# A hand-written instruction order at the two token-by-token passages of a two-layer encoder trunk

## The chip, the core and the metric

The kernel runs on one core of one Trainium2 chip. The metric is the device time of one execution, in microseconds (us). The profile is that of one execution, with the start and duration of every instruction on each engine: TensorE (PE, with its weight loads apart as PEld), VectorE (DVE), ScalarE (ACT), GpSimd (POOL) and SyncE (SP, which here only issues transfers).

## The reference

x is 256 tokens of 2048 float32 numbers. Two layers follow one another; cut to what matters here:

```python
for l in range(DEPTH):                      # 2 layers
    h = rms_norm(x, pre_mix_norm[l])
    m = hybrid_mixer(h, ...)                # h @ w_in, two kinds of attention, mix @ w_o
    x = x + rms_norm(m, post_mix_norm[l])
    h = rms_norm(x, pre_ffn_norm[l])
    f = (silu(h @ w_gate[l]) * (h @ w_up[l])) @ w_down[l]
    x = x + rms_norm(f, post_ffn_norm[l])
```

`rms_norm(m, post)` needs the sum of squares over all 2048 columns of a token before any column of it can be added to x, and the next projection needs x transposed (features on partitions). So at "output projection to gate and up" and at "down projection to the next layer's input projection" everything that follows waits for the last column of a token. The two passages occur three times: the first in both layers, the second once, between them.

## The kernel before

**Numbers.** Every float32 matrix product is made of three matmuls. Each operand is split in two: `hi`, its rounding to the matmul's format, made by ACT, and `lo`, what is left (operand minus `hi`), made by DVE. The product is hi times hi, hi times lo, and lo times hi.

**Weights.** All weights are one stream of 128x1024 pieces in the order of use (`weight_order`). `fetch(upto)` issues their transfers on SP's queue into four `raw` buffers; `feed(upto)` makes each piece's `hi` (ACT, L307) and `lo` (DVE, L317), with six buffers of each. A `hi` can be made when its raw piece has landed and PE has finished with an older piece's buffer; a raw buffer is free when its `lo` is made. In the gate and up columns after the first, some `lo` are made by POOL (`helped`, L310). Some products use a seven-product scheme for a 2x2 block (`seven_products`, L1084 to L1086, with sums of weights `T` and `G` made at L279 to L291); in the passages only plain products occur.

**Tokens.** The 256 tokens are two blocks of 128 (t = 0 and 1). The 2048 output columns of a projection are four columns c of 512. The last two columns (2 and 3) are accumulated last, and their last pairs of rows are done token block by token block: first both columns of block 0, then both of block 1, so that block 0 can be normed while PE works on block 1.

**At a passage**, for each block: an accumulator is added to a shared part (`evac_sum`, L589; in the output projection block 1's shared part was added before), ACT squares it and sums (L586, L591), DVE multiplies it by the norm's gain (L587, L592), `rescale` turns the four sums into 1/rms (ACT's Ln and Exp at L602 and L603, a Newton step in two DVE instructions, L476 and L477), and DVE adds the scaled columns to x (L627). `transposed` then turns four 128x128 parts of x on PE into one bank (L485), ACT rounds them with the next norm's gain (L488, tiles xF or xI) and DVE makes their `lo` (L493). `inv_rms` squares the new x (ACT, L512) for the next norm; the result is applied behind the next projection. The next projection's first column (gate and up: `eight`, L1250; input projection: `eight_in`, L1084 to L1086 through `product`) starts with two pairs of rows of block 0, then the same of block 1, then both blocks together. Its banks are those of the accumulators.

**Order.** A planner puts each engine's instructions in order at build time by its own estimate of when they are ready; `tc.high_priority` moves instructions forward, `tc.manual_schedule(engines=...)` keeps the written order on the named engines, `tc.issue_after(ins)` queues an instruction behind another one, and `behind()` uses that for a given number of following `lo` (the list `held`). Engines work their queue in order. Before, the output projection's passage is in written order on ACT and DVE up to block 1's last column, which is left to the planner with high priority (L1184 to L1202). The down passage (L1398 to L1420) is left to the planner, with high priority for the evacuations and rescales.

Of the kernel before, what the change touches and what calls it, by code (L numbers as in the profile page):

```python
# [17 lines left out]
P = 128  # L18
D = 2048
S = 256  # L20
L = 2
# [146 lines left out]
def kernel(  # L168
# [128 lines left out]
    def feed(upto):  # L297
        fetch(upto)
        while fed[0] < min(upto, len(stream)):
# [7 lines left out]
            nc.scalar.activation(hi, raw, AF.Copy)  # L307
# [13 lines left out]

    rests = []
    held = [None, 0]
    follows, newest_rest = {}, {}
# [154 lines left out]

    def transposed(t, g0, tiles, cols=range(4)):  # L480
        for cg in cols:
            pb = acc_bank(f"xT_ps{t}_{cg}")
            for j in range(4):
                k = cg * 4 + j
                nc.tensor.transpose(pb[:, j * P : (j + 1) * P], x_part(t, k * P, P), ident)  # L485
            for j in range(4):
                k = cg * 4 + j
                rounded = nc.scalar.activation(  # L488
                    tiles[k][:, 0, t * P : (t + 1) * P], pb[:, j * P : (j + 1) * P], AF.Copy, scale=gains[:, g0 + k : g0 + k + 1]
                )  # L490
            for j in range(4):
                k = cg * 4 + j
                rest = nc.vector.scalar_tensor_tensor(  # L493
                    out=tiles[k][:, 1, t * P : (t + 1) * P],
                    in0=pb[:, j * P : (j + 1) * P],
                    scalar=gains[:, g0 + k : g0 + k + 1],
                    in1=tiles[k][:, 0, t * P : (t + 1) * P].bitcast(F32),
                    op0=ALU.mult,
                    op1=ALU.subtract,
                )  # L500
        return rounded, rest
# [4 lines left out]
    def inv_rms(t, pool, nm, parts=None):  # L506
        ss = small.tile([P, 1], F32, tag="ssx", name=f"ssx_{nm}_{t}")
        part = small.tile([P, 4], F32, tag="ssp", name=f"ssp_{nm}_{t}")
        for h in range(4):
            if parts is None:  # L510
                junk = pool.tile([P, CW], F32, tag="t2", name=f"junk_{nm}_{t}_{h}")
                nc.scalar.activation(junk, x_part(t, h * CW, CW), AF.Square, accum_out=part[:, h : h + 1])  # L512
            else:
                nc.scalar.activation(parts[h], parts[h], AF.Square, accum_out=part[:, h : h + 1])
# [66 lines left out]

    def evac_sum(pool, acc, mg, ssm, gpost, c, t, nm, summed=False):
        m = mg[t, c // 2][:, c % 2, :]
        if summed:
            junk = pool.tile([P, CW], F32, tag="t2", name=f"jm_{nm}_{t}_{c}")
            nc.scalar.activation(junk, acc, AF.Square, accum_out=ssm[t][:, c : c + 1])  # L586
            nc.vector.tensor_tensor(out=m, in0=acc, in1=gpost[:, c * CW : (c + 1) * CW], op=ALU.mult)  # L587
            return
        nc.vector.tensor_tensor(out=m, in0=acc, in1=m, op=shared_sign(t, c % 2))  # L589
        junk = pool.tile([P, CW], F32, tag="t2", name=f"jm_{nm}_{t}_{c}")  # L590
        nc.scalar.activation(junk, m, AF.Square, accum_out=ssm[t][:, c : c + 1])  # L591
        nc.vector.tensor_tensor(out=m, in0=m, in1=gpost[:, c * CW : (c + 1) * CW], op=ALU.mult)  # L592

    def rescale(mg, ssm, t, nm, then=None, newest=None):
        halves = newest is not None
# [5 lines left out]
        nc.vector.tensor_scalar(out=half, in0=three, scalar1=-0.5 / D, scalar2=-0.5 * EPS, op0=ALU.mult, op1=ALU.add)  # L601
        nc.scalar.activation(u, fourth, AF.Ln, scale=1.0 / D, bias=most)  # L602
        nc.scalar.activation(r, u, AF.Exp, scale=-0.5)  # L603
        nc.vector.tensor_scalar(out=ms, in0=fourth, scalar1=-0.5 / D, scalar2=half, op0=ALU.mult, op1=ALU.add)
        newton(r, u, ms)
        if halves:
# [8 lines left out]
        for c in range(4):  # L615
            if halves and c == 0:
                continue
            if halves and c == 3:
# [7 lines left out]
            sl = x_part(t, c * CW, CW)  # L626
            nc.vector.scalar_tensor_tensor(  # L627
                out=sl, in0=mg[t, c // 2][:, c % 2, :], scalar=r, in1=sl, op0=ALU.mult, op1=ALU.add
            )
# [505 lines left out]
    for l in range(L):  # L1135
# [187 lines left out]
        for half in range(2):  # L1323
# [74 lines left out]
            for t in range(NT):  # L1398
# [76 lines left out]
```

## Time and profile before

| | |
|---|---|
| median of 3 runs | 2181.57 us (2181.53 to 2182.7) |
| the profiled execution, whole | 2183.48 us |
| its span in the profile | 2181.7 us |
| granted TensorE clock | 0.999 of full speed |
| PE busy | 2166.0 us (99%), 9944 matmuls |
| PEld busy | 1781.7 us (82%) |
| DVE busy | 1920.7 us (88%), 2657 instructions |
| ACT busy | 1400.4 us (64%), 2089 instructions |
| POOL busy | 260.5 us (12%) |
| DMA | 471.49 MB, mean 216 GB/s |

A row of a timeline gives the start, the duration, the engine, the line of the kernel, the operation, the tiles (output, then inputs), their shapes and the count; in brackets stands how long the engine was idle before it, and what ended that. Matmuls overlap: a row's duration is longer than the distance to the next row. A row of the waits gives who waited for whom, the total, the number of times and the longest, in us.

### The profile page before, as it was taken

To read this page: it belongs to the slowest core of one execution; us is meant where nothing else is said; L and a number is where in the kernel's file an instruction comes from. 1 tells how busy PE (TensorE), PEld (TensorE's weight loads), DVE (VectorE), ACT (ScalarE), POOL (GpSimd) and SP (SyncE) were. 2 spreads that over 40 slices of the span, in tenths; PEclk is the share of its full clock that TensorE was granted. 3 is DMA by queue.
4 is the path that set the end of the run, shared out by engine and by line. 5 is a ranking of instruction groups with operands and counts; after the bars stand their busy time and mean duration, and the time that the engine had idled before them with its cause. 6 is when DMAs were issued, how large, how long until landed. Compare 5 with 4: busy or idle time off the path is not lost.

```text
span 2181.7 us, 28784 instructions
## 1 busy us (share of the span) xinstructions
PE 2166.0 (99%) x9944; PEld 1781.7 (82%) x9944; DVE 1920.7 (88%) x2657; ACT 1400.4 (64%) x2089; POOL 260.5 (12%) x243
## 2 busy tenths in 40 slices
PE   9999999999999999999999999999999999999998
PEld 7888888788888888888878888887888888888886
DVE  7888658899999999999878886589999999999997
ACT  7666665756666656666665666657666666576664
POOL 1100000031222221000010000000212222200000
PEclk9999999999999999999999999999999999999999
DMA  9544555488887767767465555555888877768683
GB/s 323 194 164 174 193 184 176 165 300 234 239 258 229 226 231 233 239 223 258 149 241 174 172 174 188 191 164 191 286 237 241 262 222 227 240 225 244 204 268 100
DMA packets 140851, 471.49 MB, mean 216 GB/s; under 512 B 16016, under 2 KB 17040, under 8 KB 140192
## 3 DMA queue, kind: packets, MB, share of 16 engines
q1 hardware_dynamic: 121952, 436.03, 57.7%
q0 software_dynamic: 18176, 33.07, 9.2%
q8 instruction: 78, 1.28, 0.2%
q14 instruction: 69, 0.57, 0.1%
q10 hardware_dynamic: 576, 0.54, 0.1%
HBM read 461.19 MB, written 8.39 MB: 215 GB/s over the span
## 4 chain that ended last, share of the span: by engine, by line
PE 94%; DVE 3%; ACT 2%; issue 1%; DMA 0%; SPq 0%; DVEq 0%; ACTq 0%
PE c L1250 19%; PE in L1084 7%; PE in L1086 7%; PE in L1085 7%; PE dn L1357 4%; PE dn L1356 4%; PE dn L1359 4%; PE p L1085 3%; PE c L1084 3%; PE p L1084 3%; PE p L1086 3%; PE c L1085 3%; PE c L1086 3%; PE o L569 2%; PE o L571 2%; PE o L570 2%
## 5 line engine op out<-in xcount | busy, mean ns | idle before, releaser
L317 DVE TENSOR_TENSOR lo<-raw,hi 128x1024 fp32r<-128x1024 f32 x468 | 561.9, 1220 | 103.3 <-ACT hi L307 102.3
L307 ACT ACTIVATE hi<-raw 128x1024 fp32r<-128x1024 f32 x490 | 501.5, 1053 | 102.3 <-DMA raw<-in_weights_in_turn_dram 41.8
L1250 PE MATMUL c<-hi,xF 128*128 128x512 f32 x1280 | 345.9, 391 | 1.5 <-DVE xF L493 1.5
L1250 PEld LDWEIGHTS c<-hi,xF 128*128 128x128 f32 x1280 | 238.3, 188 | 50.3 <-DVE xF L493 2.0
L258 POOL DMA_DIRECT2D T<-in_weights_in_turn_dram x126 | 111.2, 883 | 1373.8 <-DMA T<-in_weights_in_turn_dram 716.6
L1250 PE MATMUL c<-lo,xF 128*128 128x512 f32 x640 | 198.2, 390 | 2.5 <-DVE lo L317 2.5
L279 ACT ACTIVATE Th<-G 128x1024 fp32r<-128x1024 f32 x126 | 133.1, 1056 | 79.8 <-DVE G L291 78.6
L281 DVE TENSOR_TENSOR Tl<-G,Th 128x1024 fp32r<-128x1024 f32 x126 | 153.9, 1221 | 10.1 <-ACT Th L279 10.1
L1356 PE MATMUL dn<-hi,jh 128*128 128x512 f32 x416 | 162.0, 389 | 0.0
L1357 PE MATMUL dn<-lo,jh 128*128 128x512 f32 x416 | 161.8, 389 | 0.0
L307 ACT ACTIVATE hi<-G 128x1024 fp32r<-128x1024 f32 x126 | 132.9, 1055 | 44.6 <-DMA G<-in_weights_in_turn_dram 27.8
L281 DVE TENSOR_TENSOR lo<-T,hi 128x1024 fp32r<-128x1024 f32 x126 | 159.6, 1266 | 0.3 <-ACT hi L279 0.2
L279 ACT ACTIVATE Th<-T 128x512 fp32r<-128x512 f32 x126 | 79.7, 633 | 118.6 <-DVE T L290 113.3
L291 DVE TENSOR_TENSOR G<-G,T 128x1024 f32<-128x1024 f32 x126 | 153.5, 1218 | 1.8
L1250 PEld LDWEIGHTS c<-lo,xF 128*128 128x128 f32 x640 | 120.1, 188 | 28.1 <-DVE lo L317 3.0
L317 DVE TENSOR_TENSOR lo<-G,hi 128x1024 fp32r<-128x1024 f32 x108 | 131.6, 1219 | 12.3 <-ACT hi L307 12.2
L279 ACT ACTIVATE hi<-T 128x1024 fp32r<-128x1024 f32 x126 | 132.2, 1049 | 12.1 <-PE c L1086 10.6
L1084 PE MATMUL in<-hi,xT 128*128 128x512 f32 x328 | 131.0, 401 | 0.6 <-DVE xT L862 0.6
L1084 PE MATMUL in<-hi,xI 128*128 128x512 f32 x328 | 131.1, 401 | 0.0
L1085 PE MATMUL in<-lo,xI 128*128 128x512 f32 x328 | 128.0, 390 | 0.3 <-DVE lo L317 0.3
L1085 PE MATMUL in<-lo,xT 128*128 128x512 f32 x328 | 127.8, 391 | 0.4 <-DVE lo L891 0.4
L1359 PE MATMUL dn<-hi,jl 128*128 128x512 f32 x416 | 128.0, 389 | 0.0
(485 smaller groups left out, 4954.2 us busy)
## 6 DMA issues: line engine op xcount, KB each, us to landing
raw<-in_weights_in_turn_dram SPq DMA_DIRECT2D x490, 512.0 KB, 4.6
T<-in_weights_in_turn_dram SPq DMA_DIRECT2D x126, 512.0 KB, 5.3
G<-in_weights_in_turn_dram SPq DMA_DIRECT2D x126, 512.0 KB, 5.4
T<-in_weights_in_turn_dram POOLq DMA_DIRECT2D x126, 256.0 KB, 6.1
GU<-in_weights_in_turn_dram SPq DMA_DIRECT2D x32, 512.0 KB, 6.5
V<-in_weights_in_turn_dram SPq DMA_DIRECT2D x8, 512.0 KB, 3.7
away_ffn<-x SPq DMA_DIRECT2D x8, 512.0 KB, 8.2
xd<-away_ffn SPq DMA_DIRECT2D x8, 512.0 KB, 9.4
```

Source lines behind the costliest of these rows:

```text
L279: nc.scalar.activation(h, w, AF.Copy)
L281: newest_rest[i] = nc.vector.tensor_tensor(out=l, in0=w, in1=h.bitcast(F32), op=ALU.subtract)
L291: nc.vector.tensor_tensor(out=g, in0=g, in1=t2.unsqueeze(1).to_broadcast([P, 2, CW]), op=ALU.add)
L307: nc.scalar.activation(hi, raw, AF.Copy)
L317: rest = nc.vector.tensor_tensor(out=lo, in0=raw, in1=hi.bitcast(F32), op=ALU.subtract)
L1084: nc.tensor.matmul(a, sh, hi, start=first, stop=False, skip_group_check=open_sums[0])
L1085: nc.tensor.matmul(a, sh, lo, start=False, stop=False, skip_group_check=open_sums[0])
L1086: return nc.tensor.matmul(a, sl, hi, start=False, stop=last, skip_group_check=open_sums[0])
L1250: nc.tensor.matmul(a, stat[part], w[j][:, kk, :], start=first and kk + n == 0, stop=last and kk == 1 and n == 2)
L1356: nc.tensor.matmul(accs[c, t], sh, hi[:, kk, :], start=first, stop=False, skip_group_check=open_sums[0])
L1357: nc.tensor.matmul(accs[c, t], sh, lo[:, kk, :], start=False, stop=False, skip_group_check=open_sums[0])
L1359: nc.tensor.matmul(accs[c, t], sl, hi[:, kk, :], start=False, stop=last, skip_group_check=open_sums[0])
```

## The change

Both passages get a written order. In the output projection's passage ACT, DVE and, for the first half, PE follow it; in the down passage of layer 0 ACT and DVE do. The steps that were one function are split (`turned_x`, `rounded_x` and `rest_of_x` out of `transposed`; `squared`, `gained` and `shared_added` out of `evac_sum`; `root_of`, which gives way at two points, and `rescaled` out of `rescale`), so that they can be interleaved one by one. `rounded_next` makes the next weight's `hi` at once and returns a function that makes its `lo` later, on DVE or on a named engine.

In the output projection: the `hi` and `lo` of the sixth weight piece of the passage stand behind the square of block 0's column 2; block 1's matmuls all come before block 0's transposes; one `lo` in each layer is made by POOL, behind the `lo` before it; block 1's gain multiplies stand behind its first two rescales, and read the accumulators until then; the squares of the next norm come behind the rounding of block 1's first columns. In the down passage of layer 0: block 0's norm follows its last column at once, the `hi` and `lo` of the next layer's first four weight pieces stand at chosen places, block 1's first rescale stands ahead of block 0's third and fourth, and the following `lo` are queued behind block 1's rests (`held_next`, two and then four of them) and two `hi` behind block 1's Exp (`rounded_behind`). All steps on the last three row pairs' activations (`prep`) come before the last pairs. The last layer's down passage keeps its order. Cut to its core:

```diff
             hi = wpool.tile([P, 2, CW], F32R, tag="hi", bufs=6, name=f"hi{i}")
-            nc.scalar.activation(hi, raw, AF.Copy)
+            with tc.issue_after(rounded_behind.pop(0).ins) if rounded_behind else nullcontext():
+                nc.scalar.activation(hi, raw, AF.Copy)
...
+    def rounded_next():
+
+        i = fed[0]
+        fetch(i + 1)
+        raw = raws[i]
+        hi = wpool.tile([P, 2, CW], F32R, tag="hi", bufs=6, name=f"hi{i}")
+        nc.scalar.activation(hi, raw, AF.Copy)
+        lo = wpool.tile([P, 2, CW], F32R, tag="lo", bufs=6, name=f"lo{i}")
+        ready[i] = (hi, lo)
+        fed[0] += 1
+
+        def rest(eng=nc.vector):
+            r = eng.tensor_tensor(out=lo, in0=raw, in1=hi.bitcast(F32), op=ALU.subtract)
+            if eng is nc.vector:
+                rests.append(r)
+            return r
+
+        return rest
...
+        if held[1] == 0 and held_next:
+            held[:] = held_next.pop(0)
...
+    def turned_x(t, cg):
+        pb = acc_bank(f"xT_ps{t}_{cg}")
+        for j in range(4):
+            nc.tensor.transpose(pb[:, j * P : (j + 1) * P], x_part(t, (cg * 4 + j) * P, P), ident)
+        return pb
...
+    def rounded_x(pb, t, cg, g0, tiles):
...
+    def rest_of_x(pb, t, cg, g0, tiles, js=range(4)):
...
-    def inv_rms(t, pool, nm, parts=None):
+    def inv_rms(t, pool, nm, parts=None, behind=None):
...
+                with tc.issue_after(behind.ins) if behind else nullcontext():
+                    nc.scalar.activation(junk, x_part(t, h * CW, CW), AF.Square, accum_out=part[:, h : h + 1])
...
+    def root_of(ssm, t, nm):
...
-        with tc.manual_schedule(engines={mybir.EngineType.Activation, mybir.EngineType.DVE}):
-            feed(idx + 6)
+        nm, g0 = f"o{l}", 32 + l * KT
+        by_hand = {mybir.EngineType.Activation, mybir.EngineType.DVE}
+        with tc.manual_schedule(engines=by_hand | {mybir.EngineType.PE}):
+            feed(idx + 5)
             for n, (c, kp) in enumerate(last_o):
                 unit({0: accs[c, 0]}, mix, idx + n, kp, (0,), False, kp == LAST_O[-1], 0)
-                if kp == LAST_O[-1]:
-                    evac_sum(pool, accs[c, 0], mg, ssm, gpost, c, 0, f"o{l}")
-            rescale(mg, ssm, 0, f"o{l}")
+                if n == 1:
+                    squared(pool, shared_added(accs[2, 0], mg, 2, 0), ssm, 2, 0, nm)
+                    feed(idx + 6)
+            gained(mg[0, 1][:, 0, :], mg, gpost, 2, 0)
+            squared(pool, shared_added(accs[3, 0], mg, 3, 0), ssm, 3, 0, nm)
+            gained(mg[0, 1][:, 1, :], mg, gpost, 3, 0)
+            rescale(mg, ssm, 0, nm)
+            rest_a = rounded_next()
+            fetch(idx + 12)
             for n, (c, kp) in enumerate(last_o):
-                feed(idx + 7 + n)
-                fetch(min(idx + 12 + n, idx + 12))
                 unit({1: accs[c, 1]}, mix, idx + n, kp, (1,), False, kp == LAST_O[-1], 0)
-                transposed(0, 32 + l * KT, xT, cols=(n,))
-                if (c, kp) == (2, LAST_O[-1]):
-                    evac_sum(pool, accs[2, 1], mg, ssm, gpost, 2, 1, f"o{l}", True)
-        with tc.high_priority(offset=URGENT):
-            evac_sum(pool, accs[3, 1], mg, ssm, gpost, 3, 1, f"o{l}", True)
-            rescale(mg, ssm, 1, f"o{l}", lambda t, c: transposed(t, 32 + l * KT, xT, cols=(c,)))
+            squared(pool, accs[2, 1], ssm, 2, 1, nm)
+            pb = [turned_x(0, cg) for cg in range(4)]
+            rounded_x(pb[0], 0, 0, g0, xT)
+            rest_of_x(pb[0], 0, 0, g0, xT, (0, 1))
+            rest_a = rest_a()
+            rest_of_x(pb[0], 0, 0, g0, xT, (2, 3))
+            rest_b = rounded_next()(nc.gpsimd)
+            tc.add_manual_dep(rest_b.ins, rest_a.ins.name, AFTER, reason="the shared port")
+            rounded_x(pb[1], 0, 1, g0, xT)
+            squared(pool, accs[3, 1], ssm, 3, 1, nm)
+            root = root_of(ssm, 1, nm)
+            next(root)
+            rest_c = rounded_next()
+            next(root)
+            rest_of_x(pb[1], 0, 1, g0, xT)
+            rest_c()
+            r = next(root)
+            rounded_next()()
+        with tc.manual_schedule(engines=by_hand), tc.high_priority(offset=URGENT):
+            rescaled(mg, 1, 0, r)
+            pb += [turned_x(1, 0)]
+            rescaled(mg, 1, 1, r)
+            pb += [turned_x(1, 1)]
+            gained(accs[2, 1], mg, gpost, 2, 1)
+            gained(accs[3, 1], mg, gpost, 3, 1)
+            turned = rounded_x(pb[4], 1, 0, g0, xT)
+            rest_of_x(pb[4], 1, 0, g0, xT)
+            rounded_x(pb[5], 1, 1, g0, xT)
+            rescaled(mg, 1, 2, r)
+            rescaled(mg, 1, 3, r)
+            rest_of_x(pb[5], 1, 1, g0, xT)
+            for cg in (2, 3):
+                rounded_x(pb[cg], 0, cg, g0, xT)
+                rest_of_x(pb[cg], 0, cg, g0, xT)
+            transposed(1, g0, xT, cols=(2, 3))
         open_sums[0] = False
-        rs = [inv_rms(t, pool, f"ffn{l}") for t in range(NT)]
+        rs = [inv_rms(t, pool, f"ffn{l}", behind=turned) for t in range(NT)]
...
+            feed(plan[l]["down"][cc[1], nkp - 1] + 1)
+            g0 = (l + 1) * KT
+
+            def added(c, t):
+                squared(pool, shared_added(accs[c, t], mg, c, t), ssm, c, t, nm)
+
+            def gain(c, t):
+                gained(mg[t, 1][:, c % 2, :], mg, gpost, c, t)
+
+            def columns(pb, t, cg):
+                return rounded_x(pb, t, cg, g0, xT), rest_of_x(pb, t, cg, g0, xT)
+
+            with tc.manual_schedule(engines=by_hand), tc.high_priority(offset=URGENT):
+                last_pairs(2, 0)
+                added(2, 0)
+                gain(2, 0)
+                root = root_of(ssm, 0, nm)
+                next(root)
+                last_pairs(3, 0)
+                added(3, 0)
+                next(root)
+                r = [next(root)]
+                rescaled(mg, 0, 0, r[0])
+                pb = [turned_x(0, 0)]
+                fetch(fed[0] + 4)
+                rounded_next()()
+                last_pairs(2, 1)
+                added(2, 1)
+                root = root_of(ssm, 1, nm)
+                next(root)
+                rounded_next()()
+                columns(pb[0], 0, 0)
+                rounded_next()()
+                rest = rounded_next()
+                last_pairs(3, 1)
+                added(3, 1)
+                rest()
+                rounded_behind[:] = [next(root)] * 2
+                rescaled(mg, 0, 1, r[0])
+                pb += [turned_x(0, 1)]
+                r += [next(root)]
+                rescaled(mg, 1, 0, r[1])
+                pb += [turned_x(1, 0)]
+                columns(pb[1], 0, 1)
+                turned, rest = columns(pb[2], 1, 0)
+                held_next[:] = [(rest, 2)]
+                rescaled(mg, 1, 1, r[1])
+                pb += [turned_x(1, 1)]
+                gain(3, 0)
+                rescaled(mg, 0, 2, r[0])
+                pb += [turned_x(0, 2)]
+                held_next.append((columns(pb[3], 1, 1)[1], 4))
+                rescaled(mg, 0, 3, r[0])
+                pb += [turned_x(0, 3)]
+                columns(pb[4], 0, 2)
+                gain(2, 1)
+                rescaled(mg, 1, 2, r[1])
+                pb += [turned_x(1, 2)]
+                columns(pb[5], 0, 3)
+                gain(3, 1)
+                rescaled(mg, 1, 3, r[1])
+                columns(pb[6], 1, 2)
+                columns(turned_x(1, 3), 1, 3)
         if l + 1 < L:
-            rs = [inv_rms(t, pool, f"in{l + 1}") for t in range(NT)]
+            rs = [inv_rms(t, pool, f"in{l + 1}", behind=turned) for t in range(NT)]
```

More of the change, by code (lines that the diff above doesn't have):

```diff
@@ L477, in newton @@
         nc.vector.scalar_tensor_tensor(out=y, in0=u, scalar=1.5, in1=y, op0=ALU.add, op1=ALU.mult)
+    def turned_x(t, cg):
[4 more added lines that the diff above has]
+    def rounded_x(pb, t, cg, g0, tiles):
+        for j in range(4):
+            k = cg * 4 + j
+            rounded = nc.scalar.activation(
+                tiles[k][:, 0, t * P : (t + 1) * P], pb[:, j * P : (j + 1) * P], AF.Copy, scale=gains[:, g0 + k : g0 + k + 1]
+            )
+        return rounded
@@ L480, in transposed @@
+    def rest_of_x(pb, t, cg, g0, tiles, js=range(4)):
+        for j in js:
+            k = cg * 4 + j
+            rest = nc.vector.scalar_tensor_tensor(
+                out=tiles[k][:, 1, t * P : (t + 1) * P],
+                in0=pb[:, j * P : (j + 1) * P],
+                scalar=gains[:, g0 + k : g0 + k + 1],
+                in1=tiles[k][:, 0, t * P : (t + 1) * P].bitcast(F32),
+                op0=ALU.mult,
+                op1=ALU.subtract,
+            )
+        return rest
     def transposed(t, g0, tiles, cols=range(4)):
@@ L481, in transposed @@
         for cg in cols:
[L482 to L500, printed above, removed]
@@ L625, in rescale @@
                 continue
[L626 to L629, printed above, removed]
+            rescaled(mg, t, c, r)
             if then is not None:
@@ new lines, in last_pairs @@
+            def last_pairs(c, t, ahead=None):
+                for kp in range(nkp - tail, nkp):
+                    tick()
+                    jh, jl = split[kp]
+                    i = plan[l]["down"][c, kp]
+                    hi, lo = ready[i] if ahead is None else weights(i, ahead)
+                    for kk in range(2):
+                        sh, sl = jh[:, kk, t * P : (t + 1) * P], jl[:, kk, t * P : (t + 1) * P]
+                        last = kp == nkp - 1 and kk == 1
+                        nc.tensor.matmul(accs[c, t], sh, hi[:, kk, :], start=False, stop=False, skip_group_check=open_sums[0])
+                        nc.tensor.matmul(accs[c, t], sh, lo[:, kk, :], start=False, stop=False, skip_group_check=open_sums[0])
+                        newest = nc.tensor.matmul(accs[c, t], sl, hi[:, kk, :], start=False, stop=last, skip_group_check=open_sums[0])
+                return [newest]
```

74 lines of the change are left out of this document (40 added, 34 removed).

## The prediction

> **What bounds the kernel now.** I read the page first, then the waits of TensorE (PE), then the timelines of PE, VectorE (DVE) and ScalarE (ACT) round the two passages, which are three stretches: the output projection to gate and up in both layers (384 and 1470 us), and the down projection to the second layer's input projection (1083 us). The page's span, and what PE waited for (total, times, longest):
>
> ```profile
> span 2181.7 us, 28784 instructions
> ...
> PE c L1250 <- DVE lo L317: 2.5, 2, 1.3
> ...
> PE c L1250 <- DVE xF L493: 1.5, 2, 0.7
> ```
>
> PE's largest waits in mid-kernel are on DVE, each twice, once a layer, and the rows below place them in these stretches. A matmul's row lasts 0.39 us but a new one starts sooner, so idle rows understate what is lost; I take the pace from the chain of waits:
>
> ```profile
> 412.18 15.24 PE c L1250 x67
> ...
> 482.72 0.88 PE actT_ps L1229 x8
> ```
>
> That is 0.227 us a matmul (15.24/67) and 0.11 us a transpose. PE's timeline in layer 0's first stretch:
>
> ```profile
> 392.57 0.39 PE L570 MATMUL o<-lo,mix_df 128*128 128x512 f32 x1
> 393.04 1.32 PE L485 MATMUL xT_ps<-ident,x 128*128 128x128 f32 x8
> 394.11 0.48 PE L571 MATMUL o<-hi,mix_df 128*128 128x512 f32 x1
> 394.43 1.26 PE L485 MATMUL xT_ps<-ident,x 128*128 128x128 f32 x8
> 396.42 1.19 PE L1250 MATMUL c<-hi,xF 128*128 128x512 f32 x4 [0.74 <-DVE xF L493]
> ...
> 403.80 1.16 PE L485 MATMUL xT_ps<-ident,x 128*128 128x128 f32 x8
> 406.21 0.50 PE L1250 MATMUL c<-lo,xF 128*128 128x512 f32 x1 [1.25 <-DVE lo L317]
> ```
>
> From 392.57 to 396.42 PE did two matmuls and 16 transposes, 2.21 us in 3.85: 1.64 lost. From 403.80 to 406.21 it did 8 transposes: 1.53 lost. Together 3.17, twice (two layers). In the down passage:
>
> ```profile
> 1088.65 0.40 PE L1084 MATMUL in<-hi,xI 128*128 128x512 f32 x1
> ...
> 1094.80 0.39 PE L1084 MATMUL in<-hi,xI 128*128 128x512 f32 x1
> 1096.56 1.98 PE L485 MATMUL xT_ps<-ident,xd 128*128 128x128 f32 x16 [1.37 <-DVE xd L627]
> ...
> 1099.06 0.40 PE L1085 MATMUL in<-lo,xI 128*128 128x512 f32 x1
> 1099.74 0.50 PE L1085 MATMUL in<-lo,xI 128*128 128x512 f32 x1 [0.29 <-DVE lo L317]
> ```
>
> 1.76 - 0.23 = 1.53 and 0.68 - 0.23 = 0.45, so 1.98. The ceiling of any reordering here is 2 x 3.17 + 1.98 = 8.3 us, 0.38%.
>
> **The change, part by part.** The amount of work is the same but for one subtraction a layer. hi is a weight's rounded part, lo its rest, xF hi and xF rest the same of the turned x. DVE and ACT rows that price them (the x4 row of L627 is token block 0's four rescales):
>
> ```profile
> 384.10 1.23 DVE L317 TENSOR_TENSOR lo<-raw,hi 128x1024 fp32r<-128x1024 f32 x1 [2.35 <-ACT hi L307]
> 385.48 1.23 DVE L317 TENSOR_TENSOR lo<-raw,hi 128x1024 fp32r<-128x1024 f32 x1 [0.16 <-ACT hi L307]
> 386.62 0.68 DVE L589 TENSOR_TENSOR mg_o<-o,mg_o 128x512 f32<-128x512 f32 x1
> 388.10 0.69 DVE L592 TENSOR_TENSOR mg_o<-mg_o,gpost_mix 128x512 f32<-128x512 f32 x1 [0.79 <-ACT jm_o L591]
> 388.70 0.68 DVE L589 TENSOR_TENSOR mg_o<-o,mg_o 128x512 f32<-128x512 f32 x1
> ...
> 391.78 0.22 DVE L476 SCALAR_TENSOR_TENSOR tot_o<-tot_o 128x1 f32<-128x1 f32 x1 [0.35 <-ACT tot_o L603]
> ...
> 392.23 2.74 DVE L627 SCALAR_TENSOR_TENSOR x<-mg_o,tot_o,x 128x512 f32<-128x512 f32 x4
> 394.89 1.22 DVE L317 TENSOR_TENSOR lo<-raw,hi 128x1024 fp32r<-128x1024 f32 x1
> 396.02 1.12 DVE L493 SCALAR_TENSOR_TENSOR xF<-xT_ps,gains,xF 128x128 fp32r<-128x128 f32 x4
> ```
> ```profile
> 391.66 1.04 ACT L307 ACTIVATE hi<-raw 128x1024 fp32r<-128x1024 f32 x1
> ```
>
> From start to start DVE spends 1.14 us on a lo (385.48 to 386.62), 0.60 on a gain multiply (388.10 to 388.70), 0.67 on a rescale (392.23 to 394.89, over four), 0.26 on an xF rest (1.12 over four, overlapped), about 0.3 on the Newton pair (0.45 with its hops, 391.78 to 392.23); ACT spends about 1.0 on a hi. Weights count from the passage's first as w0; w4 on are gate and up.
>
> *Token block 0, output projection.* w5's rounding moves behind the square of column 2. The first add can go at 385.25 (w4's lo ends) instead of 386.62; from add to multiply it is 1.48 (386.62 to 388.10), all of it add and ACT's square. But DVE now has w5's lo ahead of the multiply: 385.25 + 1.48 + 1.0 hi + 1.14 lo = 388.87, the multiply to 389.47, and the second add there instead of at 388.70. So the rescales start 0.77 later, at 393.0, and end at 395.66. If PE's hand order frees w5's buffer earlier nothing changes, as its hi stands behind the square.
>
> *PE by hand there.* All 24 matmuls of token block 1 now come before the transposes: PE ends them at 392.57 + 2 x 0.227 = 393.03, then waits for each rescale; the fourth group of transposes runs 395.7 to 396.15. The first xF rests stand directly behind the rescales (396.0), before w6's lo, so gate starts at 396.2 instead of 396.42: 0.2 won, 1.4 of the first gap stay.
>
> *Behind it.* DVE: two rests to 396.2, w6's lo 397.35, two rests 397.85, three one-column sums 398.15, four rests 399.2, then w8's lo, Newton, w9's lo, two rescales, two gains, block 1's first rest. w7's lo goes to GpSimd (POOL), held behind w6's:
>
> ```profile
> L310 POOL TENSOR_TENSOR lo<-raw,hi x22: 2400/2444/3155, 438.7 to 1895.3; 128x1024 fp32r<-128x1024 f32 x22
> ```
> ```profile
> 411.57 0.89 POOL L258 DMA_DIRECT2D T<-in_weights_in_turn_dram  x1 [261.72 <-DMA T<-in_weights_in_turn_dram]
> ...
> 444.01 2.99 POOL L310 TENSOR_TENSOR lo<-raw,hi 128x1024 fp32r<-128x1024 f32 x1 [1.43 <-ACT hi L307]
> ```
> ```profile
> 446.45 0.70 DVE L1091 TENSOR_TENSOR s<-f 128x128 f32<-128x128 f32 x1
> 447.07 0.28 DVE L1093 TENSOR_TENSOR s<-f 128x128 f32<-128x128 f32 x1
> ```
>
> It runs 397.4 to 399.85 (2.44), 400.55 at the worst (3.155). PE needs it at 396.2 + 17 x 0.227 = 400.05, so it costs 0 to 0.5; I take 0, the median. The last fence shows the price of the neighbour: a DVE operation of 0.28 us took 0.70, until the POOL one ended at 447.00. So w8's lo, due at 399.2, waits till 399.85: POOL's help saves DVE 1.14 and takes back 0.6. The Trainium skill warns of just this (Perfetto Trace Analysis, Optimizing Scalar/DVE Operations): DVE and GpSimd share an SBUF read port, so moving operations between the two might not help. Taken strictly nothing is saved; the trace agrees in that the 0.70 row was held, while the rests queued first here read PSUM on one side. On POOL's queue the w7 lo passes no transfer: the first T of the stretch, which waits for its data until 411.57, is requested only later, in the gate loop.
>
> On it goes: w8's lo to 401.0, Newton 401.3, w9's lo 402.45, two rescales 403.8, two gains (which free gate's last two banks) 405.0, first rest 405.3. Meanwhile PE has 24 matmuls to 401.65, then 12 of w8 and w9 on block 0 (w9's lo is needed at 402.8, ready at 402.45) to 404.35, and 8 transposes to 405.25. The 1.53 gap closes, with nothing to spare. So 0.2 + 1.53 = 1.75 a layer at best. Late next are w10 and w11, whose buffers block 1's matmuls free, as now.
>
> *DMA.* The loads keep their order on SP's queue; w9's waits for w5's raw buffer, now free at 388.87. With 4.6 us to land (below) it is there at 393.5, before its rounding at about 399.
>
> *Down passage.* Rounding next weights (n0, n1 ...) leaves token block 0's path:
>
> ```profile
> raw<-in_weights_in_turn_dram SPq DMA_DIRECT2D x490, 512.0 KB, 4.6
> ```
> ```profile
> 1081.03 1.06 ACT L307 ACTIVATE hi<-raw 128x1024 fp32r<-128x1024 f32 x1
> ```
> ```profile
> 1082.12 1.23 DVE L317 TENSOR_TENSOR lo<-raw,hi 128x1024 fp32r<-128x1024 f32 x1 [0.20 <-ACT hi L307]
> ...
> 1083.49 1.23 DVE L317 TENSOR_TENSOR lo<-raw,hi 128x1024 fp32r<-128x1024 f32 x1
> ...
> 1085.31 1.40 DVE L627 SCALAR_TENSOR_TENSOR xd<-mg_d,tot_d,xd 128x512 f32<-128x512 f32 x2
> ```
> ```profile
> 1095.76 2.73 DVE L627 SCALAR_TENSOR_TENSOR xd<-mg_d,tot_d,xd 128x512 f32<-128x512 f32 x4
> ```
>
> One hi and two los stood ahead of the rescale at 1085.31; without them it goes at about 1082. PE then ends the down matmuls at about 1088.1 (one group of four transposes fewer before 1088.65) and block 1's first column 18 matmuls earlier, at 1084.0. From there DVE's new queue runs: add and square 1.48 to 1085.5, hi n1 1086.5, lo n1 1087.65, four rests 1088.7, lo n2 1089.85, second add 1090.45, lo n3 1091.6, rescale (0,1) 1092.25, Newton 1092.55, rescale (1,0) 1093.2; now block 1's rescales start at 1095.76. PE wants the first rest at 1088.1 (there at 1087.95), n3's lo at 1088.1 + 16 x 0.227 = 1091.75 (there at 1091.6), and block 1 after 24 matmuls and one more group of transposes, at 1094.0. Both waits, 1.98, go, with 0.15 to spare twice. n4's and n5's los are tied behind block 1's first rests, so they come some 2.3 later than those; PE wants them 48 matmuls after 1088.1, at 1099 or later.
>
> *Free.* The eight squares for the next norm move behind a rounding; their result is used only at the end of the first gate column. What was two adjacent instructions keeps its price when split into helpers.
>
> *Sum.* At best 2 x 1.75 + 1.98 = 5.5 us. But behind the hand-ordered stretch PE's own order is the planner's, and 405.25 meets 405.3. I take off 0.3 us a passage, two thirds of the smallest wait seen (0.45): 4.6. The profiled execution took 2183.5 us round its span of 2181.7 and lies 1.9 above the median of 2181.57; less 4.6 the span is 2177.1 and the median 2177.0.
>
> **The rivals.**
> *DVE takes it back.* Later in the same gate column one place shows hardly any slack:
>
> ```profile
> 436.01 1.22 DVE L281 TENSOR_TENSOR Tl<-G,Th 128x1024 fp32r<-128x1024 f32 x1
> ```
> ```profile
> 437.44 0.39 PE L1085 MATMUL p<-Tl,sh 128*128 128x512 f32 x1
> ```
>
> Done at 437.15 (1.14 from its start), used at 437.44. An earlier PE waits there unless DVE is earlier too. DVE gains 0.54 from POOL (1.14 - 0.6) and loses the 0.77 above, so about 0.3 to 0.5 a layer stays, and 1.0 to 1.6 of the down passage: 2.1 us, 2179.5. For it: 0.29 us of slack in that row. Against: the planner moves its los with the rest, and six buffers give lead elsewhere. If nothing were saved by POOL, the layers would give 0 and the time 2180.3; that is where the Trainium skill's rule on the port (same section) leads if it holds in full.
>
> *Transposes too early (slower).* In the second half PE is not ordered by hand, and block 1's transposes are marked urgent. Placed directly behind block 0's, at 396.15, they hold PE until the second rescale at 403.8: 7.6 us against the 1.75 won, so 5.9 a layer; in the down passage transposes of (0,1) placed at 1088.1 hold it until 1092.25, 4.15 less 1.98. Both layers alone: 2 x 5.9 - 1.7 = 10.1, 2191.7; with the down passage too 14.0, 2195.6. A passage turns slower than now where its transposes stand more than 1.75 us ahead of their rescale. Against: they had the same mark before and stood 32 matmuls later, at 403.80, about when their data came.
>
> *It does nothing.* The planner's order was near this one already, or the delay of 0.77 costs what the rest wins: 2181.6.
>
> **How the numbers follow.** 0.2% is 4.4 us, about what a measurement of this kernel can tell from no change; the line is at 2177.2. Forecast case 0.58 (its own range from 2174.5, where the 0.77 goes in both layers and nothing is taken off, to 2178.2), 0.48 of it beyond the line; DVE takes it back 0.18; nothing 0.08; too early 0.16. So faster 0.48, same 0.36, slower 0.16. The range runs from 2174.5 to 2183.0, and leaves out most of the slower case.
>
> **What would show it.** Right: the waits of c on lo L317 and of the transposes on xd gone, gate's first matmul 3.4 us after the start of the last output matmul (2.3 now, with transposes between them moved ahead of it), block 1's first rescale in the down passage near 1092.5, PE's gaps there under 0.5. Wrong: a transpose row whose idle time names a rescale for several us, POOL's lo ending after PE wants it, or new waits on Tl or lo between 410 and 445.

## The result, and the profile after

The changed kernel is slower: 2190.82 us (median of 6 runs, 2189.5 to 2192.19) against 2181.99 of the kernel before (6 runs), a ratio of 1.0041 with a 95% interval of 1.003 to 1.0053. The profiled execution took 2189.77 us round a span of 2188.0 (before: 2183.48 round 2181.7), at the same granted clock of 0.999. The forecast was 2177.0, with a range to 2183.0.

The waits of TensorE after (who waited for whom, total, times, longest, in us):

```profile
PE c L1332 <- ACT hi L308: 3.4, 2, 1.7
...
PE xT_ps L506 <- DVE x L651: 1.2, 2, 0.6
PE in L1131 <- ACT xI L512: 1.0, 2, 0.7
PE p_in L1132 <- DVE Tl L281: 1.0, 1, 1.0
PE in L1133 <- DVE xI L520: 0.8, 1, 0.8
```

The two waits of before on `lo` (2.5) and xF (1.5) are gone. In their place stands a larger one, on a `hi`, again once a layer. Layer 0's place in TensorE's timeline:

```profile
413.77 0.61 PE L1332 MATMUL c<-lo,xF 128*128 128x512 f32 x2
416.07 1.20 PE L1332 MATMUL c<-hi,xF 128*128 128x512 f32 x4 [1.68 <-ACT hi L308]
```

Two matmuls in 2.30 us: 1.85 lost. ScalarE's timeline says why (L546 are the squares for the next norm):

```profile
398.75 1.04 ACT L329 ACTIVATE hi<-raw 128x1024 fp32r<-128x1024 f32 x1
403.37 4.56 ACT L512 ACTIVATE xF<-xT_ps,gains 128x128 fp32r<-128x128 f32 x17 [3.58 <-PE xT_ps L506]
407.83 0.62 ACT L546 ACTIVATE junk_ffn<-x 128x512 f32<-128x512 f32 x1
...
413.65 0.64 ACT L546 ACTIVATE junk_ffn<-x 128x512 f32<-128x512 f32 x1
...
414.95 1.07 ACT L308 ACTIVATE hi<-raw 128x1024 fp32r<-128x1024 f32 x1
```

ScalarE sits idle for 3.58 us till 403.37, then rounds the turned x, then works through the eight squares, with a few more roundings between them, from 407.83 to 414.3, and only behind them makes the `hi` that TensorE wants at 414.2.

The down passage, first on VectorE, then on TensorE (L1173: start of the shared part; L625: an accumulator's add; L651: a rescale; L1489 to L1491: the last down matmuls):

```profile
1074.54 0.69 DVE L1173 TENSOR_TENSOR mg_d<-p_d,mg_d 128x512 f32<-128x512 f32 x1 [3.51 <-PE p_d L1133]
...
1080.59 0.69 DVE L625 TENSOR_TENSOR mg_d<-dn,mg_d 128x512 f32<-128x512 f32 x1 [0.48 <-PE dn L1491]
...
1085.48 0.75 DVE L651 SCALAR_TENSOR_TENSOR xd<-mg_d,tot_d,xd 128x512 f32<-128x512 f32 x1
...
1095.98 0.75 DVE L651 SCALAR_TENSOR_TENSOR xd<-mg_d,tot_d,xd 128x512 f32<-128x512 f32 x1
```
```profile
1068.60 0.39 PE L1489 MATMUL dn<-hi,jh 128*128 128x512 f32 x1
...
1076.08 0.39 PE L1490 MATMUL dn<-lo,jh 128*128 128x512 f32 x1
1076.31 0.39 PE L1132 MATMUL dn<-Tl,jh 128*128 128x512 f32 x1
1076.53 0.39 PE L1491 MATMUL dn<-hi,jl 128*128 128x512 f32 x1
1076.76 0.39 PE L1133 MATMUL dn<-Th,jl 128*128 128x512 f32 x1
...
1088.86 0.40 PE L1491 MATMUL dn<-hi,jl 128*128 128x512 f32 x1
1089.98 0.51 PE L1131 MATMUL in<-hi,xI 128*128 128x512 f32 x1 [0.72 <-ACT xI L512]
```

The last down matmuls now start at 1068.60, among the seven products of kp 18, the pair of rows with that number (L1131 to L1133), whose last one starts at 1076.76; before it was at 1070.92. The shared part of all four accumulators needs those products, so the first add goes at 1080.59. Block 0's rescale goes at 1085.48 and not at the 1082 of the forecast. From 1060 to 1172 TensorE's gaps (the time less 0.227 us for each matmul and 0.11 for each transpose in it) are 6.7 us against 2.5 before.

TensorE's time can be cut at rows that every kernel has. The *output passage* is taken from the output projection's first matmul (tile `o`) to the first of the seven products behind it (tile `p`), *gate and up* from there to the layer's last transpose of activations (`actT_ps`), the *down stretch* from there to the first transpose behind the next layer's input projection (`qkT_ps`). The first row has the lengths before, in us; the others have the difference of the profiled execution to these:

| kernel | until layer 0's output projection | output passage, layer 0 | gate and up, layer 0 | down stretch | output passage, layer 1 | gate and up, layer 1 | span |
|---|---|---|---|---|---|---|---|
| before, length | 298.7 | 128.6 | 439.1 | 298.0 | 128.5 | 438.1 | 2181.7 |
| after | -0.6 | +0.6 | +0.9 | +4.2 | +0.6 | +0.3 | +6.3 |
| e1: output passages alone | +0.1 | +0.5 | +0.7 | 0.0 | +0.6 | +1.1 | +3.2 |
| e2: down passage alone | +0.3 | 0.0 | -0.1 | +5.1 | 0.0 | -0.6 | +4.8 |
| e3: last down matmuls behind kp 18 | +0.9 | +0.5 | -0.9 | +6.3 | +0.6 | +2.2 | +9.7 |
| e4: after, squares earlier | -0.6 | -1.5 | +0.4 | +4.4 | -1.4 | +1.2 | +2.6 |
| e5: e4, down passage as before | -0.4 | -1.5 | +2.6 | 0.0 | -1.4 | +1.0 | +0.3 |
| e6: e4, TensorE in written order in the down passage | -0.3 | -1.5 | +1.3 | +0.4 | -1.4 | +1.3 | -0.2 |
| e7: e6, no holds | -0.7 | -1.6 | +1.7 | -0.9 | -1.5 | +1.8 | -1.0 |
| e8: before, urgent mark alone | -0.4 | 0.0 | +0.3 | +9.2 | 0.0 | +0.4 | +9.7 |
| e9: before, once more | +0.2 | 0.0 | -0.6 | 0.0 | 0.0 | +1.1 | +0.9 |
| e10: e7, w7's `lo` on VectorE | +0.8 | -0.5 | +0.6 | +0.1 | -0.4 | +1.8 | +2.5 |
| e11: e7, once more | +0.6 | -1.6 | +1.6 | -0.9 | -1.5 | +0.7 | -0.9 |

The output passages repeat to 0.1 where two kernels are alike in them, and so does the down stretch in the old order (e1, e5, e9) and in e7's (e7, e11); in after's order it is 4.2 to 5.1 longer (after, e2, e4). The other stretches repeat less well: e9 is the kernel before and differs from it by up to 1.1 in one of them, and e7 and e11 are one kernel and enter the output projection 1.4 apart, ahead of everything that the change touches in layer 0. (The stretches left out, layer 1's attention and the end, add at most 0.3.) After loses 4.2 us in the down stretch and 0.6 in each output passage, where the forecast had 1.7 and twice 1.45 to win, its 0.3 a passage taken off. These profiled executions lie 6.3 apart, the medians 8.8.

### The profile page after: what moved, and what is told of

Same layout as the page of the kernel before. It is cut to its first block, busy times and chain, and to the rows that moved or that the text cites. A ratio compares the mean times of both kernels' runs of the same rounds, so it can differ in the third digit from the quotient of the medians.

```text
span 2188.0 us, 28767 instructions
## 1 busy us (share of the span) xinstructions
PE 2169.3 (99%) x9944; PEld 1780.2 (81%) x9944; DVE 1919.8 (88%) x2655; ACT 1399.2 (64%) x2089; POOL 264.7 (12%) x245
## 5 line engine op out<-in xcount | busy, mean ns | idle before, releaser
L318 DVE TENSOR_TENSOR lo<-raw,hi 128x1024 fp32r<-128x1024 f32 x456 | 546.9, 1221 | 105.8 <-ACT hi L308 104.7
L308 ACT ACTIVATE hi<-raw 128x1024 fp32r<-128x1024 f32 x478 | 487.8, 1051 | 114.1 <-DMA raw<-in_weights_in_turn_dram 47.5
L281 DVE TENSOR_TENSOR Tl<-G,Th 128x1024 fp32r<-128x1024 f32 x126 | 154.1, 1223 | 10.0 <-ACT Th L279 9.8
L281 DVE TENSOR_TENSOR lo<-T,hi 128x1024 fp32r<-128x1024 f32 x126 | 158.8, 1260 | 0.8 <-ACT hi L279 0.8
L1131 PE MATMUL in<-hi,xI 128*128 128x512 f32 x328 | 130.7, 402 | 1.0 <-ACT xI L512 1.0
L1131 PE MATMUL in<-hi,xT 128*128 128x512 f32 x328 | 131.0, 401 | 0.7 <-ACT hi L936 0.7
L1133 PE MATMUL in<-hi,xI 128*128 128x512 f32 x328 | 128.1, 393 | 0.8 <-DVE xI L520 0.8
```

Of the source, the lines that this page charges most:

```text
L281: newest_rest[i] = nc.vector.tensor_tensor(out=l, in0=w, in1=h.bitcast(F32), op=ALU.subtract)
L318: rest = nc.vector.tensor_tensor(out=lo, in0=raw, in1=hi.bitcast(F32), op=ALU.subtract)
L1131: nc.tensor.matmul(a, sh, hi, start=first, stop=False, skip_group_check=open_sums[0])
L1133: return nc.tensor.matmul(a, sl, hi, start=False, stop=last, skip_group_check=open_sums[0])
```

## The experiments

The kernel before stands beside each; its median was 2182.58 beside e1 to e4, 2184.42 beside e5 to e7, and 2183.22 beside e8 to e11.

**e1 and e2: one kind of passage alone.** e1 has the new order in the output passages and the old one in the down passage; e2 the reverse.

> The new order in the output projection's two passages alone; the down passage as before. Theory A (the down passage is what costs: the urgent mark moves its last matmuls ahead of the seven products, and the shared part comes 5 us late): the trace of the changed kernel shows the output passages 0.6 and 0.9 us slower, so 2183.5 to 2184, about 2 above before. Theory B (the squares behind the rounding in ACT's queue cost most, in each passage): two of three passages are left, so some 6 us slower, 2188. My forecast's step for these passages by itself: 3 us faster, 2179.

> The new order in the down passage alone; the output projection's passages as before. Theory A: most of the loss, 4 to 7 us slower than before, 2186 to 2189. Theory B: one passage of three, some 3 us slower, 2185. My forecast's step for this passage by itself: 1.6 faster.

e1: 2187.3 us, ratio 1.002 (1.0011 to 1.0029). e2: 2187.07, ratio 1.0021 (1.0012 to 1.003). Each part alone costs over 4 us: for e1 that is nearer to theory B, for e2 it is in the range of theory A, and both causes turn out to act. e1 has the waits on `hi` (3.4 in two), e2 the gaps of the down passage (7.6 from 1060 to 1172) and before's old waits on `lo` (2.5 in two).

**e3: the last down matmuls behind kp 18's products.** After, with all 72 queued behind the last of the seven products:

```diff
-                last_pairs(2, 0)
+                with tc.issue_after(newest_seven[0].ins):
+                    last_pairs(2, 0)
...             # the same for (3, 0), (2, 1), (3, 1)
```

> The changed kernel, but the down passage's last matmuls are queued on PE behind the last of the seven products; all else is the same. Theory A: the shared part comes at its old time, block 0's first rescale near 1082 instead of 1085.5, and the passage gives back 4 to 6 us: 2185 to 2187. Theory B: no change beyond 1 us, 2190 to 2191.

2193.25 us, ratio 1.005 (1.0037 to 1.0062): no faster than after (1.0041; the intervals overlap), where theory A had 4 to 6 us to win. Half of the reason was right. VectorE in e3:

```profile
1082.68 0.75 DVE L651 SCALAR_TENSOR_TENSOR xd<-mg_d,tot_d,xd 128x512 f32<-128x512 f32 x1
...
1093.43 0.69 DVE L625 TENSOR_TENSOR mg_d<-dn,mg_d 128x512 f32<-128x512 f32 x1 [2.72 <-PE dn L1491]
```

Block 0's rescale is at 1082.68, where the forecast had put it. But the planner now mixes the last matmuls of block 1's second column with those of the input projection, so that its add waits for them till 1093.43, and TensorE waits 1.9 for a `lo` queued behind that add. The fault moved from the first of these matmuls to the last.

**e4: the squares of the output passages earlier.** After, with block 0's squares behind block 1's Exp, where ScalarE is idle, and block 1's where they were:

```diff
-            next(root)
+            exp1 = next(root)
...
-        rs = [inv_rms(t, pool, f"ffn{l}", behind=turned) for t in range(NT)]
+        rs = [inv_rms(t, pool, f"ffn{l}", behind=(exp1, turned)[t]) for t in range(NT)]
```

> The changed kernel, but in the output projection's passages the next norm's squares of block 0 are queued behind block 1's Exp instead of behind block 1's first rounding, so that they can fill ACT's idle 3.6 us there. If the squares in front of the next weight's rounding make PE's 1.85 us gap near 414, it shrinks by the 2.6 us that four squares take, and about 1.5 to 1.9 is won in each layer: 2187 to 2188. If that rounding is late for another reason (its buffer, its transfer), nothing changes: 2190 to 2191.

2186.59 us, ratio 1.0019 (1.001 to 1.0028), against after's 1.0041. ScalarE in e4:

```profile
399.76 0.62 ACT L546 ACTIVATE junk_ffn<-x 128x512 f32<-128x512 f32 x1
...
403.43 5.31 ACT L512 ACTIVATE xF<-xT_ps,gains 128x128 fp32r<-128x128 f32 x20 [1.11 <-PE xT_ps L506]
...
412.35 1.09 ACT L308 ACTIVATE hi<-raw 128x1024 fp32r<-128x1024 f32 x1
```

Four squares fill the idle time, the `hi` is 2.6 us earlier, and the wait of c on `hi` is not in e4's list at all. The output passages, 0.6 longer in after than before, are now 1.5 and 1.4 shorter; the forecast had 1.75 at best, less 0.3. So having all eight squares ahead of that `hi` cost 2.1 us a layer, 1.85 of it in the one gap.

**e5 to e7: the down passage, with the squares as in e4.** e5 has the old down passage. e6 has the new one with TensorE in written order too, and the input projection held behind the last down matmul:

```diff
-            with tc.manual_schedule(engines=by_hand), tc.high_priority(offset=URGENT):
-                last_pairs(2, 0)
+            with tc.manual_schedule(engines=by_hand | {mybir.EngineType.PE}), tc.high_priority(offset=URGENT):
+                with tc.issue_after(newest_seven[0].ins):
+                    last_pairs(2, 0)
...             # (0, 0) is transposed behind the first six matmuls of (3, 1)
+                ended[:] = last_pairs(3, 1) * 24      # the next 24 products are issued behind it
```

e7 is e6 without `held_next` and `rounded_behind`.

> Both output passages as after but with their squares moved up (token block 0's behind block 1's Exp, block 1's behind the first rounding of its turned x), the down passage as before. Theory of the squares: the two output passages give 1.6 and 1.1 us less than before, so 2.7 below before (about 2179.5, ratio 0.9988), and the passages' own gaps on TensorE are as in the kernel with the squares moved and the new down passage. Rival (the gain of the output passages comes from where the down passage leaves the queues): same as before within 1 us.

> Squares moved, new down passage, and there TensorE too is ordered by hand: the last 72 down matmuls behind kp 18's seven products, then (2,0), (3,0), (2,1), six of (3,1), the four transposes of (0,0), twelve of (3,1), and only then the input projection. Theory A (the 4.4 us that the new down passage costs come from TensorE's order: last matmuls among kp 18's products, so that the first add goes 5 us later): token block 0's rescale goes near 1080 to 1082, block 1's second add near 1088, the gaps of 1060 to 1172 fall from 6.6 to under 3, and the time is 1 to 2 us below the kernel with the old down passage. Theory B (the rests held behind the turned x, and roundings that wait for a load, starve VectorE after 1100 in any order of TensorE): the gaps after 1095 (0.6, 1.0, 1.0, 1.1) stay, 3 to 4 us, and the time stays 2 to 4 us above the kernel with the old down passage.

> As the kernel with TensorE by hand in the down passage, but the next weights' rests are not held behind block 1's rests, and the two roundings not behind Exp. Theory A: within 1 us of the kernel that holds them. Theory B: 2 to 4 us less than it, VectorE's idle of 4.9 us near 1105 gone, and the gap of 1.1 at 1155 (Tl late) gone with it.

e5: 2183.17 us, ratio 0.9996 (0.9987 to 1.0004). e6: 2184.68, 1.0002 (0.9993 to 1.001). e7: 2183.71, 0.9997 (0.9988 to 1.0006). e5 misses the 2179.5 of its theory: its output passages are 1.5 and 1.4 shorter, as in e4, so they do not owe this to the down passage, but gate and up behind them are 2.6 and 1.0 longer. From e4 to e6 the ratio falls from 1.0019 to 1.0002 and the down stretch from 4.4 over before's to 0.4, so what the new down passage cost was mostly TensorE's order: theory A. VectorE in e6 (one line lower than after in the kernel):

```profile
1075.00 0.69 DVE L626 TENSOR_TENSOR mg_d<-dn,mg_d 128x512 f32<-128x512 f32 x1 [0.37 <-PE dn L1495]
...
1081.59 0.75 DVE L652 SCALAR_TENSOR_TENSOR xd<-mg_d,tot_d,xd 128x512 f32<-128x512 f32 x1
...
1089.13 0.68 DVE L626 TENSOR_TENSOR mg_d<-dn,mg_d 128x512 f32<-128x512 f32 x1
...
1092.09 0.75 DVE L652 SCALAR_TENSOR_TENSOR xd<-mg_d,tot_d,xd 128x512 f32<-128x512 f32 x1
```

First rescale 1081.59 (forecast about 1082), second add of block 1 1089.13 (1089.85), block 1's first rescale 1092.09 (1093.2). But e6 was not faster than e5, as theory A had it. A wait is left, which e7 takes away:

```profile
1112.98 1.08 PE L1133 MATMUL in<-hi,xI 128*128 128x512 f32 x4
1115.96 0.50 PE L1134 MATMUL in<-lo,xI 128*128 128x512 f32 x1 [1.90 <-DVE lo L319]
```

The down stretch is 0.4 longer than before's in e6 and 0.9 shorter in e7 and e11. So theory B is true for 1.3 us in the profile; in the medians e7 is 1.0 below e6, with intervals that overlap.

**e8: the urgent mark alone.** The kernel before, and only layer 0's last down matmuls marked urgent, as the change does by putting `last_pairs` inside its block:

```diff
                         for kk in range(2):
+                            with nullcontext() if l + 1 == L else tc.high_priority(offset=URGENT):
...                              # the three matmuls
```

> The kernel before, with one thing of the change: the last 72 down matmuls of layer 0 are marked urgent, as they are in the kernel after. Theory A (the mark lets these matmuls overtake kp 18's seven products, so the shared part and the first add come later): first add at 1079 to 1082 instead of 1075.5, and 2 to 5 us slower than before. Rival (the mark is harmless, the hand order of VectorE and ScalarE is what costs): same as before within 1 us.

2193.45 us, ratio 1.005 (1.0037 to 1.0062): 10.2 us slower than before, twice what theory A allowed, and the first add goes at 1085.18 where it had 1079 to 1082. VectorE, then TensorE:

```profile
1079.05 0.69 DVE L1126 TENSOR_TENSOR mg_d<-p_d,mg_d 128x512 f32<-128x512 f32 x1 [8.99 <-PE p_d L1086]
```
```profile
1096.75 1.12 PE L485 MATMUL xT_ps<-ident,xd 128*128 128x128 f32 x4 [8.87 <-DVE xd L627]
```

VectorE is idle for 8.99 us till the products that the marked matmuls overtook are done, and TensorE later stands idle for 8.87 us, when it has nothing left but the transposes. The down stretch is 9.2 longer than before's, in the changed kernel 4.2: with the new order on VectorE and ScalarE round it the same mark costs less.

**e9 to e11: where the gain stays, and GpSimd's share.** e9 is the kernel before, e11 is e7 again, e10 is e7 with w7's `lo` on VectorE:

```diff
-            rest_b = rounded_next()(nc.gpsimd)
-            tc.add_manual_dep(rest_b.ins, rest_a.ins.name, AFTER, reason="the shared port")
+            rounded_next()()
```

> The kernel before, unchanged, as one more kernel on the same chip. If the waits of p on Tl that show in the kernels with the squares moved belong to the chip, they show here too, and the gate stages of this run are as long as theirs; if they belong to the new order (VectorE is later at the matrices of the seven products when TensorE is earlier), this run has none, and its gate stages are 1 to 2 us shorter.

> As the kernel with TensorE by hand and no holds in the down passage, but in the output passages w7's lo is on VectorE again and not on GpSimd. The prediction's step (GpSimd saves VectorE 1.14 and takes 0.6 back): w8's lo 0.5 later, a wait of 0.1 to 0.5 on it in each layer, so 0.2 to 1.0 us slower than the kernel that it is made from. Rival (the port takes it all back): same within 0.2 us.

> The kernel with the squares moved, TensorE by hand and no holds in the down passage, again, beside the others on their chip. By the waits on record it lacks 4 us of before's: 2178 to 2180 if the gate stages do not give it back, 2181 to 2182 if they do.

e9: 2184.05 us, ratio 1.0004 (0.9995 to 1.0012): before against itself lies 0.8 apart in the medians, which is the size of what is left to tell. e11: 2181.62, 0.9995 (0.9986 to 1.0004). e10: 2184.76, 1.0007 (0.9998 to 1.0015), 3.1 above e11 where at most 1.0 was expected; the two intervals overlap a little, but the table has the same in the passages, 1.1 in each output passage and 1.0 in the down stretch. The waits of TensorE in e10:

```profile
PE c L1333 <- DVE xF L521: 1.9, 2, 0.9
...
PE in L1134 <- DVE lo L319: 1.3, 2, 1.1
```

The wait that comes back is the one on block 1's first rests (0.94 a layer), not on w8's `lo`. The second row is in the input projection, where e10 and e11 are written alike, and makes the 1.0 of the down stretch; why it is there in e10 and not in e11 stays open.

No version is faster than before by more than the measurement can tell: e11, e5 and e7, the best, are 0.05%, 0.04% and 0.03% below it, and all three intervals reach over 1. Yet in the profiles of e7 and e11 the three passages are together 3.9 us shorter than before's (without rounding each), of the 4.6 in the forecast. Most of that is returned in gate and up: both layers together are 3.5 longer in e7 and 2.3 in e11, and between 0.7 shorter and 0.7 longer in e2, e8 and e9, which have before's output passages. TensorE's waits of p on Tl (L281, a matrix of the seven products) are a part of it. As idle rows they are 1.7 us in e5, 1.2 in e7 and 0.2 in e11 and in e9; taken from start to start less 0.227, where that is over 0.1, they are 2.9 in e5, 2.4 in e7 and 1.5 in e11, against 0.15 before, 1.0 in e9 and 1.1 in e8. So they show in the old order too, and more in the new one, and neither theory of them is shown by itself; between e7 and e11, which are one kernel, they vary by 0.9. Where the rest is returned stays open.

## Why the prediction was wrong, step by step

- **Free: the eight squares.** Wrong, and the whole loss of the output passages. Their result was indeed not needed before the end of the column, but the step asked only who waits for their result, not what stands behind them in ScalarE's queue: the `hi` of w10. They cost 2.1 a layer (+0.6 with them, -1.5 and -1.4 with four of them moved), against a forecast of nothing. "Late next are w10 and w11, whose buffers block 1's matmuls free, as now" named the right weights with the wrong reason. The Trainium skill (PSUM — Partial Sum Buffer, section "Engine vs sequencer instructions") states the rule that was not applied: the queues of ScalarE, VectorE and GpSimd are strictly first in, first out, and matmuls run in program order. The trace agrees: the `hi` starts at 414.95, behind the last square at 413.65.
- **Down passage: "One hi and two los stood ahead of the rescale at 1085.31; without them it goes at about 1082."** Right for the queues of VectorE and ScalarE, wrong as a whole, because it took TensorE's order from before. The diff puts `last_pairs` into the urgent block, and with it its matmuls. e8 shows what that mark does alone, e6 that the forecast's times hold without it: 1.98 was to go and 4.2 came.
- **"Both waits, 1.98, go, with 0.15 to spare twice."** Even with TensorE's order set right this came only in half: in e7 and e11 a wait of 0.4 on xd is left and the stretch is 0.9 shorter. The holds, which the forecast let pass with "at 1099 or later", made a wait of 1.9 of their own in e6.
- **Token block 0: 0.77 later.** Right, though the times seem to deny it: the rescales start at 392.29, only 0.06 behind before's 392.23. But this execution had entered the output projection 0.65 earlier, at 298.01 and not 298.66, where nothing is changed yet; w4's `lo` goes 0.65 earlier with it (383.45, 384.10 before), and from there the delay is 0.7. Before:

```profile
298.66 0.48 PE L569 MATMUL o<-hi,mix_df 128*128 128x512 f32 x1
```

  After:

```profile
298.01 0.48 PE L603 MATMUL o<-hi,mix_df 128*128 128x512 f32 x1
...
392.13 0.39 PE L605 MATMUL o<-hi,mix_df 128*128 128x512 f32 x1
393.09 2.64 PE L506 MATMUL xT_ps<-ident,x 128*128 128x128 f32 x16 [0.58 <-DVE x L651]
395.49 1.17 PE L1332 MATMUL c<-hi,xF 128*128 128x512 f32 x4
```

- **Gate's start.** Right: 0.2 earlier was forecast. It is at 395.49 against 396.42, and 0.65 of these 0.93 are the earlier entry; 0.3 is won, in every kernel with the new output passages. The 3.4 from the last output matmul to gate's first came too (3.36), and with it the gap of 1.4 that was to stay (3.36 less 0.23 and 16 transposes of 0.11 is 1.37).
- **The 1.53 gap.** Closed, as forecast: the transposes of block 1 no longer stand before a missing `lo`.
- **The 0.3 a passage taken off.** Too small, 0.9 in all: of the 3.9 that the passages win in e7 and e11, the columns of gate and up behind them return 3.5 and 2.3 (0.7 either way where the output passages are before's). This is the rival "DVE takes it back" in its direction, though the waits on Tl are only a part.
- **GpSimd.** Right in direction and too small. Its `lo` took 2.42 and TensorE did not wait for it. The port took back 0.4 and not 0.6:

```profile
396.93 2.42 POOL L335 TENSOR_TENSOR lo<-raw,hi 128x1024 fp32r<-128x1024 f32 x1 [247.73 <-DVE lo L335]
```
```profile
398.80 1.62 DVE L335 TENSOR_TENSOR lo<-raw,hi 128x1024 fp32r<-128x1024 f32 x1
```

  w8's `lo` lasts 1.62 in place of 1.22, and GpSimd's ends at 399.35, while it runs. The Trainium skill's warning (Perfetto Trace Analysis, Optimizing Scalar/DVE Operations), that work moved between the two engines might not help as they share a read port, does not decide here: without GpSimd's help, in e10, the output passages are 1.1 longer.
- **The rivals.** None named the two causes. "Transposes too early" had the right side and a related mechanism (an urgent mark that moves TensorE's work), but looked at the transposes and the output passages, and these came in time; it was the mark on the matmuls. "DVE takes it back" shows in part once the two causes are out of the way, as above.

## What to carry to other kernels

An instruction whose result nobody needs soon is free only if nothing urgent stands behind it in its engine's queue: for each instruction that an edit moves, list what comes next on the same engine and when that is wanted. In this planner a mark of urgency reached every instruction written inside the block, TensorE's too, and let them overtake work that the marked instructions' own consumers needed; when ordering two engines by hand, write down what the third will do, or order it too. And before reordering for waits of 8.3 us in 2182, measure a kernel against itself: here that alone differed by 0.8, and before's median moved between 2181.6 and 2184.4 from one set of runs to the next. In a profile, compare the stretch that an edit touches from its own start to its own end, not by the clock: two executions can enter it 1.4 us apart.

## What the hardware showed that was not expected

One `lo` a layer moved back from GpSimd to VectorE made each output passage 1.1 us longer (-0.5 and -0.4 in e10 against -1.6 and -1.5 in e7 and e11). That is 2.2 of the 3.1 us between the medians (2184.76 against 2181.62). On GpSimd it saves VectorE 1.14 and holds w8's `lo` for 0.40, so 0.74 a layer was to be lost: here the instruction cost TensorE about its whole length on VectorE, as if the hold on GpSimd's side cost nothing. Why is not shown.
